# Five changes of instruction order in the two-layer hybrid encoder: merge copies and weights, last convolution, gate functions, retention's rotations, Hyena's turn

## The chip, the core and the metric

The kernel runs on one core of one Trainium2 chip. Time is device microseconds (us) of that core, as the median of repeated executions of the compiled program. One execution was recorded by the hardware profiler, and its rows are what "the trace" means below. The engines are TensorE (PE in the rows; PEld is its weight load), VectorE (DVE), ScalarE (ACT), GpSimd (POOL) and SyncE (SP, which issues most DMAs). Each engine works through its own queue in order; between engines there are semaphores.

## The reference

The reference is a trunk of two layers over an input of 512 positions by 1024 channels, all in float32.

- Layer 0: RMSNorm, one input projection, then two mixers side by side. Mixer A is a bidirectional gated DeltaNet (4 heads of 128, short convolution over three positions on q, k and v, then per chunk and direction a unit lower triangular system is solved and a state is carried from chunk to chunk). Its gates are `beta = sigmoid(b)` and `g = -exp(a_log) * softplus(a + dt_bias)`. Mixer B is a mixture of three dilated windows with rotary embedding (8 heads of 64). Both outputs go through one output projection and are added to x.
- Layer 1: RMSNorm, one input projection, then mixer C, bidirectional retention with rotary embedding (4 heads), and mixer D, Hyena: a short convolution, products, and a long convolution by Fourier transforms with filters made by a small network. Output projection, residual.
- After each layer's mixers comes RMSNorm and a feed-forward block of width 2816: gate and up projections, a convolution of three positions on the gate, `silu(gate) * up`, and a projection back. A last RMSNorm ends it.

```python
m = a + jnp.eye(C)                       # DeltaNet, per chunk: unit lower triangular
sol = lax.linalg.triangular_solve(m, rhs, left_side=True, lower=True, unit_diagonal=True)
qkv = jax.nn.silu(dwconv(proj[..., : 3 * W], conv_w))
g = -jnp.exp(a_log) * jax.nn.softplus(a + dt_bias)
x = x + conv_ffn(rmsnorm(x, norm_ffn[layer]), ...)
```

## The kernel before, in words

Dense products keep float32 accuracy by splitting each operand into a high and a low part in a matmul-friendly float32 format: `whi`/`wlo` for weights, `hh`/`hl` for activations. `mm3` (lines 263 to 267) issues three matmuls per product: high-high, high-low, low-high. A weight arrives by a 512 KB DMA on SyncE into `raw` (three buffers), ScalarE makes the high part (line 253, or line 250 where a scale is applied, as in the mixer's output projection), VectorE the low part (line 254 or 251). `fetch` does this for one weight; `get(ahead)` fetches until `ahead` weights are ready, and hands out one. There are four buffers each for high and low parts.

The text of the program does not fix the order on an engine. A planner takes every instruction with its dependencies, estimates durations, and gives each engine its queue: among the instructions that it thinks ready, the one traced first. So an instruction written later can float ahead into a gap that the planner sees, and an estimate that is off shows as a wait on the chip. Two things hold the planner: `manual_schedule`, used for the start alone, and `issue_after(ins)`, which queues what a block traces on the engine of `ins` behind `ins` on that engine; it orders the queue and waits for nothing else, and leaves the other engines' instructions free.

PSUM has two groups of four banks: `acc` for projections and outputs, `wk` for small work. A projection can start only when the reader of an older tile in its bank is done.

In order of the program, the stages that the change touches:

- **Dilated stage** (`dilated`, from line 505). Sixteen units of score, softmax, transposition (line 537, copied out at line 539 by ScalarE and VectorE in turn) and product with v (line 548). `DPROJ` says behind which unit the later q and k projections are issued, and, in its last two entries, behind which step of the loop the next piece of the generator `gates` is traced: steps 10 and 15 of 0 to 18.
- **Gates** (`gates`, from line 604). A generator in pieces: a projection of 32 columns; then four transpositions and a chain of small functions on 128 x 32 values, exponentials and logarithms on ScalarE (lines 631, 634, 639, 640, 642), the rest on VectorE; then cumulative sums by small matmuls (lines 659, 660), their exponential (line 662) and copies. The third piece is traced behind the first projection of the DeltaNet stage, since each `tile` there calls `next(gates)` (line 733).
- **DeltaNet preparation** (`delta_prep`, from line 707). Twelve projections of q, k and v columns, each with a convolution (`conv3`: ScalarE takes the middle tap at line 363, VectorE the outer taps at lines 366 and 367), Silu (lines 737 and 756), and a transposition a projection later (line 715). Then the Z projection (`proj_tok`, named `pt` in rows), in the same four `acc` banks.
- **Diagonal blocks** (`deltanet`, lines 814 to 865). The 32 x 32 diagonal blocks of the triangular systems are collected in `Bt`, transposed to `L` (line 851, VectorE), inverted by sixty dependent VectorE instructions (lines 858 and 859), and transposed back into `Y1` and `Y2` (lines 864 and 865; `vs` is the memory of `Y2`). Beside this TensorE works on the Z projection and on five units of the dilated mixer's output projection (`fill`, rows named `oacc` with `yh` and `yl`, twelve matmuls each).
- **Merge** (lines 886 to 933). Blocks of 32 are merged to 64 and then to 128: a first product (`m32`, line 890, row name `m`), its sums copied by both engines (line 892), the inverted diagonal blocks copied into `P` (line 895, eight copies, VectorE and ScalarE by direction), one filler unit, a second product (`m32b`, line 900), its sums copied (line 902); then transpositions (`vp`, lines 912 and 913) and the same for 64 (`m64`, lines 921 and 923, and `m64b`, lines 930 and 932), with another filler unit. The scan over chunks follows, with the last unit.
- **Retention** (`retention`, from line 1028). Four projections of q and k; `rope_in` copies each out of PSUM (line 458, ScalarE) and swaps halves by four DMAs on SyncE; `rope_out` multiplies and adds (lines 467 to 469, GpSimd and VectorE) and writes high and low parts (lines 474 and 475). `rot(i)` is the i-th `rope_out`. The projection of v (`pt`) follows in the same four banks.
- **Hyena** (`hyena`, from line 1212). Twelve projections (`hap`) with convolutions; u, made of the two first of each three, is transposed (`turn`, line 1240) during the third, ahead of the K step `HT`.
- **Feed-forward** (`ffn`, from line 408): 22 columns in each layer, with two projections (`gup`) each, and the projection back (`oacc`).

Of the kernel before, what the change touches and what calls it, by code (L numbers as in the profile page):

```python
# [10 lines left out]
AF = mybir.ActivationFunctionType  # L11
ALU = mybir.AluOpType
# [3 lines left out]
S = 512  # L16
# [47 lines left out]
def bc(ap, shape):  # L64
    return ap.to_broadcast(shape)


class Norm:


    out = None
# [91 lines left out]
class K:  # L163
# [194 lines left out]
    def conv3(self, out, ps, w, o, b=None):  # L358

        nc = self.nc  # L360
        w0, w1, w2 = [w[:, k:k + 1] for k in o]
        if b is None:
            nc.scalar.activation(out, ps, AF.Copy, scale=w1)
        else:
            nc.scalar.activation(out, ps, AF.Identity, scale=w1, bias=b)
        nc.vector.scalar_tensor_tensor(out[:, 1:], ps[:, :S - 1], w0, out[:, 1:], op0=ALU.mult, op1=ALU.add)
        nc.vector.scalar_tensor_tensor(out[:, :S - 1], ps[:, 1:], w2, out[:, :S - 1], op0=ALU.mult, op1=ALU.add)  # L367

    def rows_t(self, pool, srcs, nm):

# [231 lines left out]
    def gates(self, dp, n):  # L602
# [27 lines left out]
        V.tensor_scalar(e, gt[:, :, 0:8], -1.0, 80.0, op0=ALU.mult, op1=ALU.min)  # L630
        nc.scalar.activation(e, e, AF.Exp)
        V.tensor_scalar(e, e, 1.0, None, op0=ALU.add)
        nl = T("gnl")
        nc.scalar.activation(nl, e, AF.Ln)
        V.reciprocal(beta, e)
        V.tensor_tensor(y, gt[:, :, 8:16], bc(row[:, 0:1, :], [128, 4, 8]), op=ALU.add)
        V.tensor_scalar(u, y, -1.0, None, op0=ALU.mult)
        V.tensor_tensor(u, u, y, op=ALU.min)
        nc.scalar.activation(e, u, AF.Exp)
        nc.scalar.activation(row[:, 1, :], row[:, 1, :], AF.Exp)  # L640
        V.tensor_scalar(u, e, 1.0, None, op0=ALU.add)
        nc.scalar.activation(g, u, AF.Ln)
        V.tensor_scalar(u, u, -1.0, None, op0=ALU.add)
        V.tensor_scalar(g2, u, 0.0, None, op0=ALU.is_equal)
        V.tensor_tensor(u, u, g2, op=ALU.add)
# [5 lines left out]
        V.tensor_scalar(y, y, 0.0, None, op0=ALU.max)  # L651
        V.tensor_tensor(g, g, y, op=ALU.add)
        V.scalar_tensor_tensor(g, g, -1.0, bc(row[:, 1:2, :], [128, 4, 8]), op0=ALU.mult, op1=ALU.mult)
        yield
        gp = self.wk((128, 128), "gp")
        for d in range(2):
# [47 lines left out]
    def delta_prep(self, dp, n, gates, K_, Q_, V_, Z_):  # L704

        nc, I = self.nc, self.I
        V = nc.vector
        cw = self.rows_t(dp, [I["dn_conv_w"][0].rearrange("k (f p) -> (k f) p", p=128)], "dncw")
        pend = []

        def turn():
            sl, which, h = pend.pop(0)
            tp = self.wk((128, 4, 128), "tp")
            for cc in range(4):
                nc.tensor.transpose(tp[:, cc, :], sl[:, cc * 128:(cc + 1) * 128], self.ident)
            if which == 2:
                nc.scalar.copy(V_[:, :, h, :], tp)
                return
            ss = self.sm.tile([128, 4], F32, tag="dss", name="dss", bufs=2)
            jk = self.sm.tile([128, 4, 128], F32, tag="jk", name="sq", bufs=1)  # L720
            nc.scalar.activation(jk, tp, AF.Square)
            V.tensor_reduce(ss, jk, axis=AX.X, op=ALU.add)
            r = self.sm.tile([128, 4, 1], F32, tag="dr", name="dr", bufs=2)
            self.rstd(ss, 1.0, 1e-6, r[:, :, 0])
            if which == 0:
                nc.gpsimd.tensor_scalar(r, r, 128 ** -0.5, None, op0=ALU.mult)
            V.tensor_tensor((Q_, K_)[which][:, :, h, :], tp, bc(r, [128, 4, 128]), op=ALU.mult)

        def tile(which, h):
            f = which * 4 + h  # L730
            ap = self.acc(nm="ap")
            self.last_ap = self.proj_t(self.get(), n, ap).ins
            next(gates, None)
            c = self.vscr.pop(0) if which == 2 else self.s2("c")
            self.conv3(c, ap, cw, (f, 12 + f, 24 + f))
            if which < 2 or h == 0:
                nc.scalar.activation(c, c, AF.Silu)
            pend.append((c, which, h))

        for i, (which, h) in enumerate([(w_, h_) for w_ in (1, 0) for h_ in range(4)]):  # L740
            tile(which, h)
            if i:
                turn()
            if i > 5:
                yield
        tile(2, 0)
        turn()
        yield
        turn()
        tile(2, 1)  # L750
        yield
        tile(2, 2)
        yield
        tile(2, 3)
        for c, _, _ in pend:
            nc.scalar.activation(c, c, AF.Silu)
        turn()
        turn()
        yield
        turn()  # L760
        yield
        self.proj_tok(n, lambda t, a: nc.scalar.activation(Z_[:, t, :], a, AF.Silu))
        yield

    def deltanet(self, n, gates, yb, nxt):
        nc, I = self.nc, self.I
        V = nc.vector
        with ExitStack() as ctx:
# [79 lines left out]

            X = self.xp.tile([128, 32, 32], F32, tag="xn", name="L")
            Xf = X.rearrange("p a b -> p (a b)")  # L850
            V.transpose(Xf, Bt.rearrange("p m s -> p s m"))
            tm = dp.tile([128, 256], F32, name="tm")
            for _ in prep:
                pass
# [11 lines left out]
            self.x = self.new_x()  # L866
            for t in range(NT):
                self.load_x(t)
            wb = [self.get() for _ in range(4)]
            units = [(t, half) for half in range(2) for t in range(NT)]  # L870

            def fill(n):
# [15 lines left out]
            for m in range(16):  # L888
                for (d, s, o), p in zip(pairs, ps):
                    nc.tensor.matmul(p[blk(o), m, :], P[d][blk(s), m, blk(o)], Yv[d][blk(s), :, 16 * d + m], start=True, stop=True, tile_position=(32 * s, 32 * o))  # L890
            for i, ((d, s, o), p) in enumerate(zip(pairs, ps)):
                (V.tensor_copy if i % 2 else nc.scalar.copy)(T32[blk(o)], p[blk(o)])
            for q in range(4):
                for d in range(2):
                    (V.tensor_copy, nc.scalar.copy)[d](P[d][blk(q), :, blk(q)], Yu[d][blk(q), :, 16 * d:16 * d + 16].rearrange("p a m -> p m a"))
            fill(FILLS[1])
            ps = [self.wk((128, 16, 32), "m32b") for _ in pairs]
            for m in range(16):
                for (d, s, o), p in zip(pairs, ps):
                    nc.tensor.matmul(p[blk(s), m, :], T32[blk(o), m, :], Yu[d][blk(o), :, 16 * d + m], start=True, stop=True, tile_position=(32 * o, 32 * s))  # L900
            for i, ((d, s, o), p) in enumerate(zip(pairs, ps)):
                (V.tensor_copy if i % 2 else nc.scalar.copy)(P[d][blk(s), :, blk(o)], p[blk(s)])
            fill(FILLS[2])

            half = lambda b: slice(64 * b, 64 * b + 64)
# [122 lines left out]
    def retention(self, n, order):  # L1028
        nc, I = self.nc, self.I
        V = nc.vector  # L1030
        with ExitStack() as ctx:
# [8 lines left out]
            def rot(i):  # L1040
                which, s = i // 2, i % 2
                qk[which, s] = self.rope_out(rp, rope, *rin[i][:2], which == 0, f"r{which}{s}", 1)

            for i in range(4):
                if i == 3:
                    self.proj_t(self.get(), n, ps[3])
                rin.append(self.rope_in(rp, ps[i], 1.0 if i // 2 else 0.125, self.rope_room() if i % 2 else None))
                if i < 2:
                    rot(i)
            with self.tc.issue_after(rin[3][2].ins):  # L1050
                rot(2)
                rot(3)
            v = rp.tile([128, NT, 512], F32, name="rv")
            Z = rp.tile([128, NT, 512], F32, name="rz")
            self.proj_tok(n, lambda t, a: nc.scalar.copy(v[:, t, :], a))
# [274 lines left out]

WB = 4
TPD = lambda k: k.acc
DPROJ = (0, 2, 5, 8, 10, 15)
DAT = (1, 2)
FILLS = (5, 1, 0, 1, 0, 0, 0, 0, 1)
VT = (0, 1)
# [1 line left out]
G4 = 10  # L1338
FILLC = 1
IA = 3  # L1340
HT = 6
HSKIP = (1, 3)


# [56 lines left out]
```

## Time and profile before

| | |
|---|---|
| median of 3 runs | 1330.83 us (1330.3 to 1331.14) |
| the profiled execution | 1330.02 us |
| its span, first to last instruction | 1328.2 us |
| VectorE, ScalarE, GpSimd busy | 750.6, 531.6, 147.4 us |
| mean granted TensorE clock | 0.996 |
| DMA | 123.61 MB, mean 93 GB/s |

A row of a timeline gives the start, the duration, the engine, the line of the kernel, the operation, what it writes and reads, and the shape; in square brackets the idle time of the engine before it, and what ended that. A row of a group gives a count, the busy time, the mean duration in ns, and the idle time before. A row of waits gives who waited for whom, the total in us, the number of times and the longest. A row of a stretch (A:B) gives the length and the busy time of each engine, then the granted TensorE clock as a share, the DMA share and GB/s. Matmuls overlap: one of 512 columns lasts 0.39 us in the rows, and the next starts 0.23 us after it. The name behind an arrow is the releaser that came last by the profile, and can be wrong where that engine had long been done.

### The profile page before, as it was taken

To read this page: it belongs to the slowest core of one execution; us is meant where nothing else is said; L and a number is where in the kernel's file an instruction comes from. 1 tells how busy PE (TensorE), PEld (TensorE's weight loads), DVE (VectorE), ACT (ScalarE), POOL (GpSimd) and SP (SyncE) were. 2 spreads that over 40 slices of the span, in tenths; PEclk is the share of its full clock that TensorE was granted. 3 is DMA by queue.
4 is the path that set the end of the run, shared out by engine and by line. 5 is a ranking of instruction groups with operands and counts; after the bars stand their busy time and mean duration, and the time that the engine had idled before them with its cause. 6 is when DMAs were issued, how large, how long until landed. Compare 5 with 4: busy or idle time off the path is not lost.

```text
span 1328.2 us, 17628 instructions
## 1 busy us (share of the span) xinstructions
PE 1304.8 (98%) x6977; PEld 1093.2 (82%) x6977; DVE 750.6 (57%) x1085; ACT 531.6 (40%) x840; POOL 147.4 (11%) x176
## 2 busy tenths in 40 slices
PE   7999999999999999999999999999999999999997
PEld 6877788878988888888889787888898888888886
DVE  6777559957754433444436837869754442244432
ACT  4566648344433331233326424442443331133332
POOL 3354120003000000000001200124100000000002
PEclk9999999989999999999999999999999999999999
DMA  7531113411333333333323513330243333333321
GB/s 219 129 94 36 51 32 96 143 49 60 93 113 96 95 95 95 96 95 97 98 91 101 162 48 92 102 94 18 67 140 95 95 95 96 87 117 98 95 79 64
DMA packets 161025, 123.61 MB, mean 93 GB/s; under 512 B 6985, under 2 KB 134477, under 8 KB 160944
## 3 DMA queue, kind: packets, MB, share of 16 engines
q1 hardware_dynamic: 160798, 122.43, 31.2%
q8 instruction: 55, 0.90, 0.3%
q14 instruction: 26, 0.21, 0.1%
q10 hardware_dynamic: 146, 0.07, 0.0%
HBM read 117.23 MB, written 2.10 MB: 90 GB/s over the span
## 4 chain that ended last, share of the span: by engine, by line
PE 84%; DVE 7%; ACT 4%; issue 2%; DMA 1%; POOL 1%; SPq 0%; POOLq 0%; ACTq 0%; DVEq 0%
PE gup L266 11%; PE gup L265 11%; PE gup L267 11%; PE oacc L265 7%; PE oacc L267 7%; PE oacc L266 7%; PE hap L267 2%; PE pt L265 2%; PE hap L265 2%; PE hap L266 2%; PE pt L267 2%; PE pt L266 2%; PE ap L267 1%; PE ap L265 1%; PE ap L266 1%
## 5 line engine op out<-in xcount | busy, mean ns | idle before, releaser
L254 DVE TENSOR_TENSOR wlo<-raw,whi 128x1024 fp32r<-128x1024 f32 x191 | 236.0, 1237 | 304.1 <-ACT whi L253 299.3
L253 ACT CAST whi<-raw 128x1024 fp32r<-128x1024 f32 (+1 forms) x197 | 206.7, 1050 | 427.6 <-PE gup L266 186.8
L265 PE MATMUL gup<-hh,whi 128*128 128x512 f32 x656 | 255.2, 389 | 0.0
L266 PE MATMUL gup<-hl,whi 128*128 128x512 f32 x656 | 255.2, 389 | 0.0
L267 PE MATMUL gup<-hh,wlo 128*128 128x512 f32 x656 | 255.2, 389 | 0.0
L267 PEld LDWEIGHTS gup<-hh,wlo 128*128 128x128 f32 x656 | 123.1, 188 | 25.6
L265 PEld LDWEIGHTS gup<-hh,whi 128*128 128x128 f32 x656 | 123.2, 188 | 25.6
L266 PEld LDWEIGHTS gup<-hl,whi 128*128 128x128 f32 x656 | 123.2, 188 | 25.4
L265 PE MATMUL oacc<-whi,ghi 128*128 128x512 f32 x352 | 137.1, 389 | 0.0
L267 PE MATMUL oacc<-whi,glo 128*128 128x512 f32 x352 | 137.0, 389 | 0.0
L266 PE MATMUL oacc<-wlo,ghi 128*128 128x512 f32 x352 | 136.9, 389 | 0.0
L267 PEld LDWEIGHTS oacc<-whi,glo 128*128 128x128 f32 x352 | 66.1, 188 | 13.7
L265 PEld LDWEIGHTS oacc<-whi,ghi 128*128 128x128 f32 x352 | 66.1, 188 | 13.7
L266 PEld LDWEIGHTS oacc<-wlo,ghi 128*128 128x128 f32 x352 | 66.1, 188 | 13.6
L430 DVE TENSOR_TENSOR sl<-gup,sl 128x512 f32<-128x512 f32 x42 | 29.0, 692 | 81.8 <-PE gup L267 81.8
L315 DVE TENSOR_TENSOR x<-oacc,x 128x512 f32<-128x512 f32 x64 | 43.4, 685 | 49.3 <-PE oacc L267 49.2
L429 ACT ACTIVATE sl<-c 128x512 f32<-128x512 f32 x44 | 27.8, 632 | 89.2 <-DVE c L367 89.2
L265 PE MATMUL first<-hh,whi 128*128 128x256 f32 x192 | 54.9, 288 | 0.0
L266 PE MATMUL first<-hl,whi 128*128 128x256 f32 x192 | 54.5, 284 | 0.2 <-DVE hl L226 0.2
L267 PE MATMUL first<-hh,wlo 128*128 128x256 f32 x192 | 54.3, 283 | 0.0
L265 PE MATMUL pt<-whi,hh 128*128 128x512 f32 x128 | 50.2, 392 | 2.6 <-ACT room L458 1.7
L104 POOL TENSOR_SCALAR ss<-ss 128x1 f32<-128x1 f32 x16 | 5.0, 312 | 429.3 <-ACT jk L102 429.3
(422 smaller groups left out, 2346.4 us busy)
## 6 DMA issues: line engine op xcount, KB each, us to landing
raw<-in_ffn_w_in_dram SPq DMA_DIRECT2D x88, 512.0 KB, 3.8
raw<-in_ffn_w_out_dram SPq DMA_DIRECT2D x44, 512.0 KB, 3.9
raw<-in_ab_w_in_dram SPq DMA_DIRECT2D x28, 512.0 KB, 3.9
raw<-in_cd_w_in_dram SPq DMA_DIRECT2D x24, 512.0 KB, 4.3
x<-in_x_dram SPq DMA_DIRECT2D x16, 256.0 KB, 5.0
raw<-in_ab_w_out_dram SPq DMA_DIRECT2D x8, 512.0 KB, 3.8
raw<-in_cd_w_out_dram SPq DMA_DIRECT2D x8, 512.0 KB, 3.8
rs<-rt SPq DMA_DIRECT2D x32, 64.0 KB, 2.0
```

Of the source, the lines that this page charges most:

```text
L104: nc.gpsimd.tensor_scalar(ss[:, 1:2], ss[:, 0:1], s, EPS, op0=ALU.add, op1=ALU.add)
L253: self.nc.scalar.copy(hi, raw)
L254: (self.nc.gpsimd if self.pool_lo else self.nc.vector).tensor_tensor(lo, raw, hi, op=ALU.subtract)
L265: mm(out, a[0], b[0], start=start, stop=False)
L266: mm(out, a[0], b[1], start=False, stop=False)
L267: return mm(out, a[1], b[0], start=False, stop=stop)
L315: self.nc.vector.tensor_add(xs, acc, xs)
L429: nc.scalar.activation(sl, c, AF.Silu)
L430: nc.vector.tensor_mul(sl, up, sl)
```

## The change

No arithmetic changes. It has these parts:

1. Gates: the logarithm of `e` works on a copy (VectorE) and stands behind the other functions; `DPROJ` ends in 18 instead of 15, so that the second piece is traced behind the whole dilated stage; one more `yield` lets the third piece follow the second projection of the DeltaNet stage instead of the first.
2. Last convolution: the transposition to `L` is queued behind the last instruction of the last convolution, on VectorE.
3. Merge: the diagonal copies are queued behind the copies of the first sums on both engines, and VectorE takes six of the eight; the fourth `get` for the filler units asks for one weight ahead instead of two, and two `fetch` calls, queued behind the copies of the second sums, take its place and that of the next.
4. Retention: ScalarE's part of `rot(1)` is queued behind the copy of the fourth projection, as that of `rot(2)` and `rot(3)` was.
5. Hyena: `HT` is 7 instead of 6.

```diff
-        nc.vector.scalar_tensor_tensor(out[:, :S - 1], ps[:, 1:], w2, out[:, :S - 1], op0=ALU.mult, op1=ALU.add)
+        return nc.vector.scalar_tensor_tensor(out[:, :S - 1], ps[:, 1:], w2, out[:, :S - 1], op0=ALU.mult, op1=ALU.add)
...
-        nl = T("gnl")
-        nc.scalar.activation(nl, e, AF.Ln)
         V.reciprocal(beta, e)
...
+        nl = T("gnl")
+        V.tensor_copy(nl, e)
         nc.scalar.activation(e, u, AF.Exp)
         nc.scalar.activation(row[:, 1, :], row[:, 1, :], AF.Exp)
         V.tensor_scalar(u, e, 1.0, None, op0=ALU.add)
         nc.scalar.activation(g, u, AF.Ln)
+        nc.scalar.activation(nl, nl, AF.Ln)
...
+        yield
         yield
         gp = self.wk((128, 128), "gp")
...
-            self.conv3(c, ap, cw, (f, 12 + f, 24 + f))
+            self.last_conv = self.conv3(c, ap, cw, (f, 12 + f, 24 + f)).ins
...
-            V.transpose(Xf, Bt.rearrange("p m s -> p s m"))
+            with self.tc.issue_after(self.last_conv):
+                V.transpose(Xf, Bt.rearrange("p m s -> p s m"))
...
-            wb = [self.get() for _ in range(4)]
+            wb = [self.get(1 + (i < 3)) for i in range(4)]
...
-            for i, ((d, s, o), p) in enumerate(zip(pairs, ps)):
-                (V.tensor_copy if i % 2 else nc.scalar.copy)(T32[blk(o)], p[blk(o)])
-            for q in range(4):
-                for d in range(2):
-                    (V.tensor_copy, nc.scalar.copy)[d](P[d][blk(q), :, blk(q)], Yu[d][blk(q), :, 16 * d:16 * d + 16].rearrange("p a m -> p m a"))
+            out = [(V.tensor_copy if i % 2 else nc.scalar.copy)(T32[blk(o)], p[blk(o)]).ins
+                   for i, ((d, s, o), p) in enumerate(zip(pairs, ps))]
+            with self.tc.issue_after(out[2]), self.tc.issue_after(out[3]):
+                for q in range(4):
+                    for d in range(2):
+                        (nc.scalar.copy if d and q % 2 else V.tensor_copy)(P[d][blk(q), :, blk(q)], Yu[d][blk(q), :, 16 * d:16 * d + 16].rearrange("p a m -> p m a"))
...
-            for i, ((d, s, o), p) in enumerate(zip(pairs, ps)):
-                (V.tensor_copy if i % 2 else nc.scalar.copy)(P[d][blk(s), :, blk(o)], p[blk(s)])
+            out = [(V.tensor_copy if i % 2 else nc.scalar.copy)(P[d][blk(s), :, blk(o)], p[blk(s)]).ins
+                   for i, ((d, s, o), p) in enumerate(zip(pairs, ps))]
+            with self.tc.issue_after(out[2]), self.tc.issue_after(out[3]):
+                for _ in range(2):
+                    self.fetch()
...
-                if i < 2:
+                if i == 0:
+                    rot(0)
+            with self.tc.issue_after(rin[3][2].ins):
+                for i in range(1, 4):
                     rot(i)
-            with self.tc.issue_after(rin[3][2].ins):
-                rot(2)
-                rot(3)
...
-DPROJ = (0, 2, 5, 8, 10, 15)
+DPROJ = (0, 2, 5, 8, 10, 18)
...
-HT = 6
+HT = 7
```

## The prediction

> **What bounds the kernel.** I read the page first, its span, busy times and costliest groups.
>
> ```profile
> span 1328.2 us, 17628 instructions
> PE 1304.8 (98%) x6977; PEld 1093.2 (82%) x6977; DVE 750.6 (57%) x1085; ACT 531.6 (40%) x840; POOL 147.4 (11%) x176
> L254 DVE TENSOR_TENSOR wlo<-raw,whi 128x1024 fp32r<-128x1024 f32 x191 | 236.0, 1237 | 304.1 <-ACT whi L253 299.3
> L265 PE MATMUL gup<-hh,whi 128*128 128x512 f32 x656 | 255.2, 389 | 0.0
> ```
>
> TensorE has work in 98% of the span. The change removes no matmul, so all it can win is TensorE's waiting, some 23 us, and whatever TensorE does more slowly around a wait. So the next view is that of waits, for TensorE, matmuls first and then weight loads:
>
> ```profile
> PE m32b L900 <- DVE s L892: 1.9, 2, 1.4
> PE pt L265 <- ACT room L458: 1.7, 1, 1.7
> PE m32b L900 <- ACT s L892: 1.2, 1, 1.2
> PE pt L265 <- DVE scr L367: 0.9, 1, 0.9
> PE op L548 <- ACT pT L539: 0.9, 1, 0.9
> PE tp L1240 <- ACT hsh L225: 0.6, 1, 0.6
> ```
> ```profile
> PEld m L890 <- DVE vs L865: 0.4, 1, 0.4
> ```
>
> Six rows, five places, 7.2 us: merge sums, retention's fourth projection, the last convolution, the gates' functions, the hyena turn. Each edit points at one of them. The seventh row matters as much: when the merge starts, TensorE is already waiting for VectorE's transposed inverse, so time won shortly ahead of it may be handed back there.
>
> The sum is made against the profiled execution, 1330.02 us (span 1328.2 and 1.8 around it). That is 0.8 below the median of the three runs, 1330.83, so the total is carried over with 0.8 added.
>
> **Gates.** ScalarE at the end of the dilated stage (start, duration):
>
> ```profile
> 134.39 1.28 ACT L634 ACT_TABLE_LOAD   x1
> 135.68 0.23 ACT L634 ACTIVATE gnl<-ge 128x32 f32<-128x32 f32 x1
> 135.93 1.28 ACT L639 ACT_TABLE_LOAD   x1
> 137.36 0.57 ACT L539 COPY pT<-tp 128x512 f32<-128x512 f32 x1
> ```
>
> The last probabilities' copy (L539) stands behind two table loads and three small functions, and the last product waits 0.9. DPROJ's 18 puts the second piece of the gates behind all of the stage, and the copy of e with a late Ln makes Exp, Exp, Exp, Ln, Ln of what was Exp, Ln, Exp, Exp, Ln: two of 1.28 us loads fewer. The copy then finds ScalarE free: -0.9. The added tensor_copy is one of VectorE's small ones, hidden beside the projections. The piece's four transposes merely move behind the products. Its two loads of eight values on SyncE move with it; at worst they lengthen a chain that now has a whole projection (24 matmuls of 0.23, 5.5) to spare. Who is late next? The extra yield moves the cumulative sums and their Exp from behind the first projection to behind the second, and with them a pair of table switches:
>
> ```profile
> 150.33 0.63 ACT L737 ACTIVATE scr<-scr 128x512 f32<-128x512 f32 x1
> ```
> ```profile
> 152.79 0.60 PE L715 MATMUL tp<-ident,scr 128*128 128x128 f32 x4
> ```
>
> Today Silu ends at 150.96 and its reader starts at 152.79: 1.8 to spare. One projection later a Square of 0.6 comes in between; 1.2 remains, so I take nothing. Bounds: -0.9, and +0.5 if the turn gives back 1.4 (below).
>
> **Last convolution.** VectorE, at the start and at the end of its elimination chain; then TensorE:
>
> ```profile
> 228.91 2.06 DVE L851 STREAM_TRANSPOSE L<-Bt 128x1024 f32<-128x1024 f32 x1
> 262.43 1.21 DVE L865 STREAM_TRANSPOSE vs<-L 128x1024 f32<-128x1024 f32 x1
> ```
> ```profile
> 263.97 0.23 PE L890 MATMUL m<-Y,P 32*32 32x32 f32 x2
> ```
>
> The transposition of 2.06 was queued ahead of the convolution's second half, which holds a PSUM buffer that the Z projection wants. Swapped, the buffer is free some 2 us earlier and TensorE's 0.9 goes. But VectorE does the same two instructions in the same time, so its sixty-step elimination starts and ends as before; vs is ready at 263.64 and m starts at 263.97. TensorE arrives 0.9 earlier and waits 0.9 longer. I take 0; ends 0 and -0.9 (if a filler unit of the output projection is pulled ahead of m).
>
> **Merge.** The largest term. First the stretches 270 to 275 and 275 to 280 with the granted clock (third column from the right), then groups of VectorE, TensorE and ScalarE from the start of m to the end of m64b, 263.9 to 286:
>
> ```profile
> 270.00:275.00 5.00, 2.96 (x129) 2.61 (x130) 3.59 (x5) 1.14 (x3) 0.24 (x1) 0.72 0.44 135
> 275.00:280.00 5.00, 4.83 (x38) 2.90 (x37) 1.88 (x5) 1.86 (x6) 0.80 (x1) 0.60 0.27 105
> ```
> ```profile
> L315 DVE TENSOR_TENSOR x<-oacc,x 128x512 f32<-128x512 f32 x5 | 3.4, 683 | 1.0 <-PE oacc L267 0.9
> L251 DVE SCALAR_TENSOR_TENSOR wlo<-raw,dnw,whi 128x1024 fp32r<-128x1024 f32 x2 | 2.6, 1278 | 0.7 <-ACT whi L250 0.7
> L895 DVE COPY P<-vs 32x512 f32<-32x512 f32 x4 | 2.4, 602 | 0.0
> L913 DVE COPY s<-vp 64x256 f32<-64x256 f32 x4 | 1.5, 417 | 3.1 <-PE vp L912 3.1
> L892 DVE COPY s<-m 32x512 f32<-32x512 f32 x2 | 1.4, 693 | 0.1
> L902 DVE COPY P<-m32b 32x512 f32<-32x512 f32 x2 | 1.4, 692 | 1.3 <-PE m32b L900 1.3
> ```
> ```profile
> L895 ACT COPY P<-Y 32x512 f32<-32x512 f32 x3 | 3.4, 1128 | 0.0
> ```
> ```profile
> 271.12 1.42 DVE L892 COPY s<-m 32x512 f32<-32x512 f32 x2
> ```
> ```profile
> 274.52 0.80 PE L265 MATMUL oacc<-whi,yh 128*128 128x512 f32 x1
> 280.07 2.36 PE L921 MATMUL m<-s,P 64*64 64x64 f32 x64
> 282.36 0.50 PE L265 MATMUL oacc<-whi,yh 128*128 128x512 f32 x1
> 283.95 2.08 PE L930 MATMUL m64b<-P,s 64*64 64x64 f32 x64
> ```
>
> m is done at about 265.9, but its sums are copied by VectorE only at 271.12, behind four diagonal copies, two weights' low halves (L251) and x additions. TensorE stands idle 3.1 us, and behind that the granted clock falls to 0.72 and 0.60: a filler's matmul takes 0.80, where those of gup take 0.39.
>
> Afterwards the sums go first, while the filler unit of twelve matmuls runs, so m32b has no wait and there is no reason for the lower clock. What bounds then? Of the eight diagonal copies VectorE gets six (was four), since ScalarE needs 1.13 for one. Its queue from the end of m to what the first half of m64 reads: sums 2 x 0.69, diagonals 6 x 0.60, one addition 0.68, L902 2 x 0.69, the two weights 2 x 1.28, now directly ahead of L913, and two L913 at 0.42: 10.5. With 0.3 of hand-overs m64 starts at 265.9 + 10.8 = 276.7, not 280.07: -3.4. The six filler matmuls between m64 and m64b (282.36 to 283.95, 1.6) are by then spent, in time that TensorE has to spare; I keep 0.4 for the wait that they covered: -1.2. Together -4.6. ScalarE's two diagonals and two weights are shorter than this. Bounds: -2.0, if the weights and diagonals hold L913 up for another 2.6 (two more weights' worth); -6.5, if neither the wait (3.1) nor the low clock (5 x 0.28 and 5 x 0.40, so 3.4) leaves anything.
>
> The weights prepared here are wanted only by the mixer's output projection past 316, so lateness costs nothing; SyncE's raw loads behind them move some 5 us, with FFN weights due far later.
>
> **Retention.** ScalarE, and TensorE's row behind it:
>
> ```profile
> 735.48 1.26 ACT L474 CAST r<-rt 64x512 fp32r<-64x512 f32 x2 [2.49 <-DVE rt L469]
> 738.90 1.26 ACT L474 CAST r<-room 64x512 fp32r<-64x512 f32 x2 [1.08 <-DVE room L469]
> 740.18 0.60 ACT L458 ACTIVATE room<-rqk 128x512 f32<-128x512 f32 x1
> ```
> ```profile
> 740.83 0.50 PE L265 MATMUL pt<-whi,hh 128*128 128x512 f32 x1 [1.68 <-ACT room L458]
> ```
>
> L458 frees the PSUM buffer. It stands behind rotation 1's casts, which wait for VectorE. With those queued behind it, it has only rotation 0's casts ahead, to 736.7, and ends at 737.3; TensorE wants it at 740.83 - 1.68 = 739.1, and even a weight's cast of about a microsecond in between would not make it late: -1.7. The four DMAs on SyncE that follow L458 go 2 to 5 us earlier. Rotation 1's cast becomes late by one instruction of 0.6; heads 2 and 3 read it twenty microseconds on. Bounds -1.7, and -1.0 if VectorE's or ScalarE's order leaves 0.7.
>
> **Hyena turn.** VectorE, then TensorE:
>
> ```profile
> 884.88 0.68 DVE L1254 TENSOR_TENSOR u<-vx 128x512 f32<-128x512 f32 x1
> ```
> ```profile
> 885.70 0.52 PE L1240 MATMUL tp<-ident,u 128*128 128x128 f32 x3 [0.64 <-ACT hsh L225]
> ```
>
> The page names hsh, but u ends at 885.56, just ahead of tp: VectorE is what it waits for. HT 7 puts three more matmuls (3 x 0.23) ahead: -0.6. Bounds -0.6, and 0 if u is pushed back as far as tp.
>
> **Sum.** 0.9 + 0 + 4.6 + 1.7 + 0.6 = 7.8. 1330.02 - 7.8 = 1322.2; with 0.8, 1323.0.
>
> **Rivals.** *VectorE eats the merge.* Only 2.0 there: the wait moves from m32b to vp and m64. For: the queue above makes VectorE the bound already, and two of its copies more in ahead would do it. Against: over the same stretch, to 280.07, VectorE took 14.2, with 3.1 of idling at L913 that the new order fills. Gain 5.2, 1325.6.
> *Fillers cover all.* The filler is pulled ahead of m, so the convolution's 0.9 stays won and TensorE bounds the merge: 0.9 + 0.9 + 6.5 + 1.7 + 0.6 = 10.6, 1320.2. Against: VectorE's 10.5 queue doesn't shrink when TensorE is early.
> *Table switches reach the second projection.* If ScalarE needed two more 1.28 between Exp and Silu, 2.6 against 1.2 to spare, the turn waits 1.4: 1324.4. Against it: in the rows each function starts 1.29 after its load starts. [...]
> *Orders elsewhere shift.* The planner builds each engine's queue from estimated times, so five edits can move others; a new wait of over 5 cancels the gain: about 1330. For: rows such as L851's place show it estimates wrongly by a microsecond. Against: the stages between have no wait now.
> *Slower: FFN columns.* A moved weight preparation (1.24) lands ahead of a column's additions and recurs in 44 columns. It decides from 0.18 a column (7.8 in all); at 0.25 it is 11, so 1334. Against: gup's 656 matmuls have 0.0 idle before them, and VectorE is idle 304 us at L254 alone.
> *Not done as said* would be an order already in force; the trace shows each of the five orders otherwise, so none.
>
> **Numbers.** Forecast 0.50, VectorE 0.20, fillers 0.12, switches 0.05, orders elsewhere 0.08, FFN 0.05. The likeliest gives 1323.0, by itself 1321 to 1325. The range takes in the first four: below, the fillers' 10.6 and 0.1 for each of the five restarts (0.50 for 0.39 in retention's row), 11.1, 1319.7; above, the VectorE case with retention and the turn at their small ends (0.9 + 2.0 + 1.0 = 3.9, 1326.9). About 0.2% (2.7 us) is what a measurement can tell: faster 0.87, same 0.08, slower 0.05.
>
> **What would show it.** Right: no L458, L367 or L539 row among TensorE's waits; L892 directly behind m on both engines; clock 1.00 through the merge; m still waiting on L865, now by 0.9 longer; m64 some 3.4 earlier relative to m. Wrong: L913 standing behind L251 for over 3 us, a wait at gp or at the second turn, idle before gup, or a halved clock again.

## The result, and the profile after

The changed kernel takes 1322.37 us (median of 6 runs, 1322.2 to 1322.88), the kernel before 1330.99 beside it (6 runs, 1330.3 to 1332.83): a ratio of 0.9933, 95% interval 0.992 to 0.9946. The profiled execution took 1322.2 us, 7.8 less than that of before. The granted clock differs between executions, and the time with it: 32 further executions of the kernel before took 1328.5 to 1328.8 us at 0.998, 1329.0 to 1330.8 at 0.996 or 0.997, and 1332.0 to 1332.9 at 0.993 or 0.994, while all six of the changed kernel had 0.998 or 0.999.

Line numbers behind the gates' functions are 2 to 7 higher from here on: m is L893, the sums' copies L894, the diagonal copies L899, m32b L904, vp L919, m64 L928, m64b L937; the edits of an experiment shift them by a few more.

From the page of the changed kernel, its span and busy times (the work is what it was):

```profile
span 1320.1 us, 17630 instructions
PE 1302.8 (99%) x6977; PEld 1092.6 (83%) x6977; DVE 751.6 (57%) x1088; ACT 527.1 (40%) x837; POOL 146.4 (11%) x176
```

Rows of TensorE's waits in the changed kernel (us in total, times, longest). Of the five places that the prediction went for, three are gone from the view, and the two others have shrunk: the merge's wait has moved on to vp, at 0.2, and the Hyena turn (L1247) has 0.2 left. m now waits visibly for vs:

```profile
PE tp L537 <- ACT pT L539: 0.8, 1, 0.8
PE vnp L973 <- DVE s L959: 0.6, 1, 0.6
PE m L893 <- DVE vs L868: 0.4, 1, 0.4
PE vp L919 <- DVE P L905: 0.2, 1, 0.2
PE tp L1247 <- ACT hsh L225: 0.2, 1, 0.2
```

(The wait at L537 is not the one of the gates: it ends at 83.4 us, in the first part of the dilated stage, and was 0.8 before the change too.) The stretches that answer to those shown of before, with the granted clock third from the right:

```profile
265.00:270.00 5.00, 5.00 (x142) 3.98 (x140) 4.85 (x9) 3.43 (x5) 0.41 (x1) 1.00 0.02 3
270.00:275.00 5.00, 4.80 (x44) 2.90 (x42) 4.40 (x6) 4.01 (x7) 0.63 (x1) 1.00 0.35 109
275.00:280.00 5.00, 5.00 (x123) 4.68 (x124) 3.70 (x8) 1.72 (x3) 0.41 (x1) 1.00 0.73 209
```

The clock is whole throughout, and TensorE is busy for 14.8 of these 15 us. Rows of VectorE through the merge, in order of time (diagonal copies and additions to x between them are left out):

```profile
261.14 1.20 DVE L868 STREAM_TRANSPOSE vs<-L 128x1024 f32<-128x1024 f32 x1
264.46 1.42 DVE L894 COPY s<-m 32x512 f32<-32x512 f32 x2 [0.35 <-PE m L893]
270.20 1.42 DVE L905 COPY P<-m32b 32x512 f32<-32x512 f32 x2
272.12 0.42 DVE L920 COPY s<-vp 64x256 f32<-64x256 f32 x1 [0.50 <-PE vp L919]
272.57 2.48 DVE L251 SCALAR_TENSOR_TENSOR wlo<-raw,dnw,whi 128x1024 fp32r<-128x1024 f32 x2
275.08 1.08 DVE L920 COPY s<-vp 64x256 f32<-64x256 f32 x3
```

The sums are copied at 264.46, directly behind m, where they came at 271.12 before. But the two weights (L251) stand between the first copy of vp and the other three. What that does shows on TensorE, where m64 runs in two pieces:

```profile
274.89 1.14 PE L928 MATMUL m<-s,P 64*64 64x64 f32 x16
276.40 2.07 PE L928 MATMUL m<-s,P 64*64 64x64 f32 x48
278.31 2.08 PE L937 MATMUL m64b<-P,s 64*64 64x64 f32 x64
```

Where the time came from is read by setting the starts of the same instructions on TensorE beside each other; where the difference grows, time was won. The two traces start their first projection at 15.51 and 15.59, so 0.08 is put to the gates' row. (Differences are taken before rounding.)

| TensorE's instruction | before | after | difference | won since the row above |
|---|---|---|---|---|
| first projection behind the dilated stage | 139.42 | 138.02 | -1.39 | 1.47 (gates) |
| last of the Z projection | 250.05 | 247.88 | -2.18 | 0.79 (convolution) |
| first filler matmul behind m | 265.90 | 264.40 | -1.50 | -0.68 (given back at m) |
| start of m64 | 280.07 | 274.89 | -5.18 | 3.68 (merge) |
| start of m64b | 283.95 | 278.31 | -5.64 | 0.46 (merge) |
| first product of retention | 761.85 | 754.19 | -7.66 | 1.99 (retention; 0.03 on the way) |
| end of the Hyena projections | 887.09 | 879.02 | -8.07 | 0.41 (HT) |

### The profile page after: what moved, and what is told of

It reads as the page before. It is cut to its first block, busy times and chain, and to the rows that moved or that the text cites. A ratio compares the mean times of both kernels' runs of the same rounds, so it can differ in the third digit from the quotient of the medians.

```text
span 1320.1 us, 17630 instructions
## 1 busy us (share of the span) xinstructions
PE 1302.8 (99%) x6977; PEld 1092.6 (83%) x6977; DVE 751.6 (57%) x1088; ACT 527.1 (40%) x837; POOL 146.4 (11%) x176
## 4 chain that ended last, share of the span: by engine, by line
PE 87%; DVE 6%; ACT 2%; DMA 1%; issue 1%; SPq 1%; POOL 1%; POOLq 0%; ACTq 0%; DVEq 0%
PE gup L266 11%; PE gup L267 11%; PE gup L265 11%; PE oacc L266 7%; PE oacc L267 7%; PE oacc L265 7%; PE pt L267 2%; PE pt L265 2%; PE pt L266 2%; PE first L266 2%; PE first L267 2%; PE first L265 1%; PE ap L266 1%; PE ap L265 1%; PE ap L267 1%; PE hap L265 1%
```

## Experiments

Every kernel below is the changed one with the edit that its diff shows. Times are medians of 5 runs (10 for e2). The interval of a ratio is some 1.7 us to either side, so differences of half a microsecond between these kernels are read from the traces, and the times only say whether they fit. Where two traces are set on each other, the start of the first projection (15.59 in the changed kernel) is taken out. In e2 and e7 that isn't all: there 0.6 and 0.3 us more are lost before anything that the edits touch (in e7 the first projection behind the dilated stage starts at 138.39, 0.37 later than in the changed kernel, of which 0.10 is there at the start); why isn't shown.

**e2, all of the merge undone.**

```diff
-            wb = [self.get(1 + (i < 3)) for i in range(4)]
+            wb = [self.get() for _ in range(4)]
...
-            with self.tc.issue_after(out[2]), self.tc.issue_after(out[3]):
...
-                        (nc.scalar.copy if d and q % 2 else V.tensor_copy)(P[d][blk(q), ...
+                        (V.tensor_copy, nc.scalar.copy)[d](P[d][blk(q), ...
...
-                for _ in range(2):
-                    self.fetch()
```

> Undone: all edits of the merge (sums copied in program order with the diagonal blocks, four of these on each engine, weights fetched ahead of the merge as before). Theory (the merge is worth what TensorE's milestones shifted by between the start of m and the end of m64b, 4.1): 1326.5, within 0.4, with m32b waiting about 3 again and the granted clock below 1 in the stretch behind it. Rival (part of that shift is the convolution's 0.9, which could only be used because the merge became shorter): +5.0, 1327.4.

Measured: 1326.46, ratio to before 0.9974 (0.9964 to 0.9983), so 4.1 above the changed kernel. In the trace m64b comes 4.66 later (282.97 for 278.31), of which 0.3 is there already at the filler unit behind m. The waits at m32b are back, and the low clock with them:

```profile
PE m32b L903 <- DVE s L895: 1.9, 2, 1.5
PE m32b L903 <- ACT s L895: 1.4, 1, 1.4
```
```profile
270.00:275.00 5.00, 3.69 (x129) 2.83 (x129) 3.55 (x6) 1.15 (x2) 1.04 (x1) 0.62 0.45 134
```

The merge is half of the whole gain, and its gain is its own: the time is the theory's 1326.5 and not the rival's 1327.4, so the convolution's share isn't in it. Its edits are two, the place of the weights and the place of the diagonal copies; e3 and e4 keep one each.

**e3, only the copies' order** (weights fetched ahead of the merge again: `wb` as in e2, the two `fetch` gone).

> Only half of the merge's edits: the sums stay ahead of the diagonal blocks (and six of these on VectorE), but the two weights are fetched ahead of the merge as before, so both low halves (2 x 1.24) stand ahead of the sums on VectorE. Theory (the filler unit of 4.7 gives the queue slack, and either edit alone takes enough out of the way of the sums): sums copied by about 268.3, ahead of m32b's start at 269.2; vp starts some 2.4 later than in the changed kernel, but its copies no longer stand behind the weights, so m64 ends at about the same time: 1322.4, within 0.6. Rival (the two edits add up, about half of 4.1 each): 1324.4.

Measured: 1326.31, 0.9967 (0.9955 to 0.998): by the median nothing is left of the merge's gain, and both expectations fall. But the profiled execution is the quickest of the five, 1324.86 at a clock of 0.998 (the others took 1325.18, at 0.998, and 1326.31 to 1326.92, at 0.996 or 0.997), so its trace covers 2.7 (1324.86 beside the changed kernel's 1322.2) of the 3.9 that lie between the medians; the rest goes with a lower clock that no trace of this kernel shows. VectorE of this kernel:

```profile
262.64 1.27 DVE L251 SCALAR_TENSOR_TENSOR wlo<-raw,dnw,whi 128x1024 fp32r<-128x1024 f32 x1
264.42 1.29 DVE L251 SCALAR_TENSOR_TENSOR wlo<-raw,dnw,whi 128x1024 fp32r<-128x1024 f32 x1
266.34 1.42 DVE L894 COPY s<-m 32x512 f32<-32x512 f32 x2
272.90 1.42 DVE L905 COPY P<-m32b 32x512 f32<-32x512 f32 x2
```

The sums are there at 267.8 (266.34 + 1.42), by the theory's 268.3, and m32b waits 0.4 for them, where the theory had no wait. But everything behind is 2.7 later (L905 at 272.90 for 270.20), and vp waits for it:

```profile
274.37 0.67 PE L916 MATMUL vp<-ident,P 64*64 64x64 f32 x16 [2.46 <-DVE P L905]
275.96 3.89 PE L925 MATMUL m<-s,P 64*64 64x64 f32 x64
```

Then came what the theory had left out. It expected that the copies of vp, with no weights between them, would make up for the 2.4. They came in time, but m64 took 3.89 where it takes 2.36 at the whole clock (its row in e11, below): three stretches, one during it and a short one on either side, show the clock at 1.00, 0.50 and 1.00 again.

```profile
275.80:276.10 0.30, 0.30 (x6) 0.21 (x5) 0.30 (x2) 0.30 (x1) 0.00 (x0) 1.00 0.00 0
276.20:279.50 3.30, 3.30 (x62) 3.30 (x61) 0.97 (x2) 0.58 (x1) 0.00 (x0) 0.50 0.00 0
279.70:280.00 0.30, 0.30 (x4) 0.23 (x3) 0.11 (x1) 0.20 (x1) 0.00 (x0) 1.00 0.00 0
```

So 2.7 of late copies became a wait of 2.46, and behind the wait came a clock that cost 1.5 more; part of both is covered by filler matmuls, and m64b starts 3.1 later than in the changed kernel.

**e4, only the weights' place** (diagonal copies as in e2, in program order, four on each engine).

> The other half: the two weights stay behind the sums of m32b, but the diagonal blocks are copied in program order again, four on each engine, ahead of the sums of m. Theory (the filler unit covers them): on VectorE the sums end at about 267.9, on ScalarE, behind four copies of 1.13, at about 266.9, both ahead of m32b's start at 269.2; so 1322.4, within 0.5, no wait at m32b. Rival (the copies ahead of the sums are what held m32b up, as the change's own words have it): about +2, 1324.4, with m32b waiting on the sums.

Measured: 1322.73, 0.9942 (0.993 to 0.9955): nearly all of the gain is there. ScalarE, then VectorE, of this kernel (its trace lies 0.86 later from the first projection on):

```profile
261.99 4.44 ACT L898 COPY P<-Y 32x512 f32<-32x512 f32 x4 [11.39 <-DVE Y L867]
266.45 1.18 ACT L895 COPY s<-m 32x512 f32<-32x512 f32 x2
```
```profile
267.40 1.42 DVE L895 COPY s<-m 32x512 f32<-32x512 f32 x2
```

The sums stand behind the diagonal copies on both engines, and are done at 267.6 and 268.8 all the same, when TensorE comes out of the filler unit at 268.1. m32b waits 0.44, where the theory had no wait, and m64b is 0.4 later than in the changed kernel (1.23 less the 0.86). So of the merge's two edits the weights' place brings some 4 by itself, and the copies' order 0.4 on top of it. Without the weights' place the order brings nothing by the medians (1326.31 for 1326.46), and 1.8 between the two profiled executions, 0.5 of which lies ahead of m; whether the rest is the copies or the clock isn't shown, since e2's trace has 6.8 us at half clock and e3's 3.4.

**e10, e2 with TensorE kept busy.** Diff against e2:

```diff
             fill(FILLS[1])
+            p = self.acc(nm="warm")
+            for _ in range(24):
+                nc.tensor.transpose(p[:, :128], self.ident, self.ident)
```

> The kernel with all the merge's edits undone (1326.5 in its own run), plus 24 transpositions of the identity that nobody reads, between the filler unit and m32b: some 3 us of TensorE work in the time in which it waits for the sums. Work is added, nothing moved. Theory (the loss in the merge is the wait for the copies; the halved clock behind it is hidden by VectorE's queue but for some 0.5): the granted clock stays at 1.00 and the time falls by 0.3 to 0.7, to 1325.8 to 1326.2. Rival (the lower clock is itself a large part of the loss, up to the 3.4 of the prediction's bound): 1323 to 1325.

Measured: 1324.98, 0.9955 (0.9942 to 0.9967), a span of 1324.1 beside e2's 1324.8. TensorE, and then the stretches:

```profile
267.23 2.78 PE L902 MATMUL warm<-ident 128*128 128x128 f32 x24
270.58 0.22 PE L906 MATMUL m32b<-vs,s 32*32 32x32 f32 x1 [0.36 <-DVE s L895]
271.30 0.22 PE L906 MATMUL m32b<-Y,s 32*32 32x32 f32 x1 [0.44 <-DVE s L895]
```
```profile
273.00:273.30 0.30, 0.30 (x17) 0.21 (x7) 0.04 (x1) 0.08 (x1) 0.00 (x0) 1.00 0.16 44
273.40:276.70 3.30, 3.30 (x10) 1.76 (x9) 1.25 (x2) 1.34 (x3) 1.04 (x1) 0.50 0.45 161
276.80:277.10 0.30, 0.30 (x11) 0.28 (x11) 0.00 (x0) 0.00 (x0) 0.00 (x0) 1.00 0.03 14
```

The waits at m32b shrink to 0.8, since work that is of no use to anybody stands in their place, and the halved clock to one stretch of 3.4 (e2's stretches read 0.50 from 271.30 to 277.90, and 1.00 up to 271.10 and from 278.10 on). Neither expectation holds wholly: the clock of the theory did not stay at 1.00, and the median gained 1.5, just inside the rival's 1323 to 1325. The profiled execution, the longest of its five, gained 0.8, of which only 0.36 lies between the filler unit behind m and m64b (17.92 for e2's 18.28). Two of the five were granted 0.999, as most of the changed kernel's, and took 1324.98 and 1325.3: 1.2 to 1.5 less than e2's median and 2.6 to 2.9 more than the changed kernel's. So the larger part of the merge's 4.1 is the queue of copies (with the added work in it), and the lower clock is some 1.2 to 1.5 of it. That is an estimate, since no trace of those two executions was kept.

**e11, the weights later still.**

The two `fetch` move from behind the copies of m32b to behind the second pair of copies of m64b, `out` being these:

```diff
-            with self.tc.issue_after(out[2]), self.tc.issue_after(out[3]):
-                for _ in range(2):
-                    self.fetch()
...
+            with self.tc.issue_after(out[0]), self.tc.issue_after(out[1]):
+                for _ in range(2):
+                    self.fetch()
```

> The two weights are fetched behind the copies of m64b instead of behind those of m32b; all else as changed. Their low halves (2.5 on VectorE) then no longer stand between the copies of vp, so m64 runs in one piece. Theory (TensorE has filler work in that time and is busy for 4.8 of the 5 us there, so little is left to win): 1322.0 to 1322.4, m64b 0.2 to 0.5 earlier. Rival (VectorE still holds up the merge, the prediction's 1.2 between m64 and m64b of which 0.5 came): -0.7 or more, 1321.6, m64b 0.7 earlier or more. Rival on the other side (the weights now stand ahead of the copies of sp, in the scan): +0.5 to +2.

Measured: 1322.58, 0.9936 (0.9924 to 0.9948), the same as the changed kernel. The trace shows that both rivals came true at once, with opposite signs:

```profile
273.19 2.36 PE L925 MATMUL m<-s,P 64*64 64x64 f32 x64
277.06 2.08 PE L934 MATMUL m64b<-P,s 64*64 64x64 f32 x64
282.58 2.02 PE L983 MATMUL sp<-s,s 128*128 128x128 f32 x16 [1.45 <-ACT s L975]
```
```profile
279.78 2.19 ACT L250 ACTIVATE whi<-raw,dnw 128x1024 fp32r<-128x1024 f32 x2
281.88 1.05 ACT L975 COPY s<-vnp 128x512 f32<-128x512 f32 x2
```

m64 runs in one piece and starts 1.70 earlier, m64b 1.25 (277.06 for 278.31): the two weights did hold the merge up. This move takes their 2.2 on ScalarE (L250) out of the way of the copies of vp along with the 2.5 on VectorE (L251), so it doesn't tell the two engines apart. Then the weights' high halves (L250) stand ahead of the copies of vnp on ScalarE, and the scan waits 1.45 for them; at the scan's end the kernel is 0.34 behind. The wait is moved, not removed.

**e5, e6, e7: the gates' three edits.** e5 undoes the place (DPROJ 15, one `yield`), e6 the order of the functions, e7 takes out the extra `yield` alone. The edits of e5 and of e6:

```diff
-DPROJ = (0, 2, 5, 8, 10, 18)
+DPROJ = (0, 2, 5, 8, 10, 15)
...
-        yield
```
```diff
+        nl = T("gnl")
+        nc.scalar.activation(nl, e, AF.Ln)
         V.reciprocal(beta, e)
...
-        nl = T("gnl")
-        V.tensor_copy(nl, e)
...
-        nc.scalar.activation(nl, nl, AF.Ln)
```

> Of the gates' edits only the order of the functions stays (Exp, Exp, Exp, Ln, Ln); the piece goes back to its old place in the dilated stage (DPROJ 15) and the extra step between it and the sums is gone. Theory (the place is what frees the last probabilities' copy): one table load of 1.28 and two functions still stand ahead of that copy on ScalarE, which starts by some 137.1 instead of 137.4 before the change, so 0.6 to 0.9 of the wait stays; +0.7 to +1.2, 1323.1 to 1323.6. Rival (the two table loads fewer are what counts): +0.2 at most, 1322.6.

> The other half: the piece stays behind the dilated stage (DPROJ 18, extra step), but the functions run as before, Exp, Ln, Exp, Exp, Ln, with two table loads of 1.28 more in the piece. Theory: the gates' chain ends 2.6 later, at about 147.1, and its reader gp comes at 149.6, so nothing waits: 1322.4, within 0.3. Rival (table switches reach the second projection: the turn or gp waits): +0.5 to +1.4, with a wait at gp or at the turn's tp.

> Only the extra step is taken out: the gates' cumulative sums gp stand one projection earlier on TensorE, at about 143.3, all else as changed. Theory (the gates' chain, now behind the dilated stage, ends at 144.5 on VectorE, so gp comes too early for it): TensorE waits about 1.2 at gp; +1.2, 1323.6. Rival (the step only moved work that nobody waits for): 0, 1322.4.

Measured: e5 1322.87 (0.9937, 0.9924 to 0.9951), e6 1322.23 (0.9933, 0.992 to 0.9945), e7 1322.72 (0.9937, 0.9924 to 0.9949). One row of TensorE's waits for each, of e5, e6 and e7:

```profile
PE op L548 <- ACT pT L539: 0.7, 1, 0.7
```
```profile
PE tp L716 <- ACT scr L738: 0.2, 1, 0.2
```
```profile
PE gp L660 <- DVE gg L654: 0.3, 1, 0.3
```

In e5 the wait for the last probabilities' copy is back at 0.7 of its 0.9, and the projections start 0.9 later (0.81 plus the 0.07 by which this trace is early), as the theory had it; the time lies between theory and rival. In e6 they start where the changed kernel's do. So the place alone frees the copy. The order alone, with two table loads of 1.28 fewer (three in the gates' functions before, L634, L639 and L642; one in the changed kernel, L643), wins 0.6 of the 1.47 that both won together, of which only 0.2 is waiting; with the place changed it adds nothing there. In e6 the second turn, which has 1.5 to spare in the changed kernel (Silu ends at 149.47, the turn starts at 150.96), waits 0.2, and the projections end 0.45 later (0.39 and 0.05): the rival of the table switches is real, but small. In e7 gp waits 0.3, not the 1.2 that the theory forecast, because the first projection ends at 144.1, its transpositions (rowp) included, and not at 143.3, and the planner put one more matmul and a transposition ahead of gp, which starts at 144.97; the projections end 0.7 later (0.77, less 0.10), of which 0.3 is the difference at the start and 0.4 lies behind gp.

**e1, the convolution undone** (the `issue_after(self.last_conv)` line).

> Undone: the convolution's second half no longer goes ahead of the block transposition (the transposition is issued without waiting for it); all else as in the changed kernel. Theory (the 0.9 that TensorE no longer waits at the Z projection is handed back at m, where VectorE's transposed inverse vs is next late): 0.9 of waiting behind L367 comes back, the wait of m on vs shrinks from 0.4 to nearly nothing, and the end moves by 0 to +0.3: 1322.4 to 1322.7. Rival (the conversion of this wait is a gain of its own): +0.8, so 1323.2, with m's wait unchanged.

Measured: 1322.57, 0.9942 (0.9928 to 0.9955). The wait behind the convolution is back, in TensorE's waits, and m's is gone from them:

```profile
PE pt L265 <- DVE scr L367: 1.0, 1, 1.0
```

The Z projection ends 0.76 later than in the changed kernel (0.74 and 0.02), and at m32b only 0.09 of that is left. What is won there is handed back at m, as the theory has it.

**e8, retention undone** (`rot(1)` ahead of the fourth read again), **e9, HT back at 6.**

> Undone: retention's rotation 1 stands ahead of the fourth projection's read of its sums again. Theory (that read, L458, frees the PSUM buffer for the projections behind it, and is held up by the casts of rotation 1): the wait behind L458 of 1.7 returns, and with the weight load and restart around it TensorE's milestones shift by 2.0: 1324.4, within 0.3. Rival (the prediction's size, the wait alone): 1324.1; rival (other work fills the place): 1322.4.

> Undone: HT back at 6, so three matmuls fewer stand ahead of the hyena turn. Theory: the wait at that turn returns to 0.6 from 0.2, so +0.4 there, and at the end 1322.4 to 1322.8. Rival (the prediction's size): +0.6, 1323.0. Both are below what five rounds resolve in the time; the turn's wait in the trace decides.

Measured: e8 1323.89, 0.9948 (0.9935 to 0.996); e9 1322.51, 0.9935 (0.9922 to 0.9947). The wait of each in TensorE's view, e8 and then e9:

```profile
PE pt L265 <- ACT room L458: 1.7, 1, 1.7
```
```profile
PE tp L1247 <- ACT hsh L225: 0.6, 1, 0.6
```

In e8 the first product of retention comes 1.99 later (1.82, and the trace is 0.17 early by then). In e9 the turn's wait is 0.6 instead of 0.2, and the end of the Hyena projections moves by 0.37 from where they start: both traces as the theory had them. e8's time, 1.5 above the changed kernel's, falls 0.2 short of the theory's range; e9's can't tell.

**e12, four edits alone:** the weights' place, the gates' place with its step, retention, HT.

> Only four edits stay: the weights behind the sums of m32b, the gates' piece with its extra step behind the dilated stage, retention's rotation behind the fourth read, HT at 7. Undone together: the convolution ahead of the transposition, the sums ahead of the diagonal blocks with their 6 to 2 division, and the order of the gates' functions. Theory (each of these three brought 0.4 or less by itself): 1322.4 to 1323.1. Rival (they cover for each other, and without all of them the waits of before come back): 1324 or more.

Measured: 1323.13, 0.994 (0.9927 to 0.9954). Its waits show the three edits that are missing, each at its own place and none over 0.9:

```profile
PE pt L265 <- DVE scr L367: 0.9, 1, 0.9
PE m32b L901 <- DVE s L893: 0.4, 1, 0.4
PE tp L716 <- ACT scr L738: 0.2, 1, 0.2
```

TensorE ends 0.95 later than in the changed kernel; the sum of the three single ones (e1 0.34, e4 0.44, e6 0.29) is 1.07. They do not cover for each other: four edits bring 7.2 to 7.9 by the medians (1323.13 beside 1330.37 and 1330.99), and the other three the rest, which the medians alone can't resolve. No kernel among the twelve is measurably quicker than the changed one.

## Why the prediction was right

**What bounds, and the list of places:** right. Five places of waiting were named, and the time came from those five and the stretch of low clock; no other stage moved by more than 0.15.

**Gates, 0.9 forecast:** 1.47 came. The step was right and a term was missing: the product behind the wait also ran slowly. It took 1.43 before the change (the last sixteen matmuls) where its neighbours take 1.09; afterwards two such products run in one go. Before, and then after:

```profile
135.97 1.09 PE L548 MATMUL op<-pT,dv 128*64 128x128 f32 x16
137.98 1.43 PE L548 MATMUL op<-pT,dv 128*64 128x128 f32 x16 [0.91 <-ACT pT L539]
```
```profile
135.68 1.97 PE L548 MATMUL op<-pT,dv 128*64 128x128 f32 x32
138.02 0.48 PE L265 MATMUL ap<-hh,whi 128*128 128x512 f32 x1
```

Row by row: the last 32 matmuls went from 3.44 (135.97 to 139.41) to 1.97, so 1.47 was won: 0.91 of idle time, 0.34 of slow running, and 0.22 because one run of 32 takes less than two of 16 (1.97 for twice 1.09). The slow running isn't part of every wait, and its cause is not shown: in e5, behind 0.72 of waiting, the last sixteen take 1.09. The two table loads were put down as part of this gain; e6 shows that with the new place they belong elsewhere, to the second turn, for which the prediction took nothing because 1.2 remained. With the new order that is right; without it 0.2 of waiting comes in (e6), so the loads removed are what keeps the turn free.

**Last convolution, 0:** right, for the reason given (e1). TensorE reaches m 0.54 ahead of the end of vs, where it came 0.33 behind it, so 0.87 earlier against it; forecast was 0.9. One reading was off: that TensorE was already waiting for vs before the change. The row is one of a weight load, and its 0.4 was hidden: m started 0.32 behind the start of the last filler matmul (263.65 to 263.97), as m32b does in the changed kernel (267.03 to 267.35), where nothing waits.

**Merge, 4.6:** 4.14 came, by 3.68 at m64 (forecast 3.4) and 0.46 up to m64b (forecast 1.2). The second term was mis-sized: the six filler matmuls are spent ahead, as forecast, but m64 itself now stands in two pieces behind L251. The first term's size came out (from the start of the filler unit behind m, 264.40, to m64 it is 10.5; the prediction had 10.8 from the same point, 265.9), but its reason was half right. The prediction let the sums' place ahead of the diagonal blocks remove m32b's wait, with the weights as the queue's other part; e4 and e3 show that moving the weights is all but enough (m32b still waits 0.44), and that moving the sums alone leaves the medians where they were. With the weights ahead, VectorE's copies are late by 1.9 (the sums) to 2.7 (those of m32b) even so, and the wait only goes from m32b to vp. That the two weights set the start of m64 is borne out by e11 (1.70 earlier without them there); that it is VectorE's half of them, as the prediction has it, fits the second piece of m64, which starts 0.24 behind VectorE's last copy of vp (276.16), but isn't shown: the first piece stands behind vp and filler matmuls with no wait ahead of it.

**Retention, 1.7:** 1.99, again more than the idle time of 1.68. The rows count idle time from the end of the matmul ahead, but the next one normally starts 0.23 behind its start, and here it came 2.06 behind (738.77 to 740.83), and the one after 0.34 behind that. **Hyena turn, 0.6:** 0.41, since u is pushed back a little too: 0.18 of waiting stays.

**The sum:** 7.8 against 7.8 between the two profiled executions (8.1 between their spans). That is better than its terms, and so in part luck: gates and retention were 0.9 too low together, the merge and the turn 0.7 too high. The median came out 0.6 below the 1323.0 of the prediction, and the two medians lie 8.6 apart: the 0.8 that was carried over, as if both kernels' medians lay above their profiled executions alike, holds only for the kernel before, whose executions spread more.

**Rivals.** VectorE eating the merge is the nearest one in its mechanism (the weights hold up vp and m64, as e11 shows), but the new order is short enough that filler work hides it. The fillers did not move ahead of m, so the convolution's 0.9 did not stay. The table switches cost 0.2 at the turn in e6, not the 1.4 of the prediction. The FFN columns did not move: gup's first matmul and retention's come 5.67 earlier alike.

What stays open is the share of the halved clock in the merge. It is some 1.2 to 1.5 by e10, which also changes the waiting. The kernel before gives the same figure: those of its executions that were granted 0.998 took 1328.5 to 1328.8, 1.2 to 1.5 less than the profiled 1330.02 at 0.996. But where in them the clock was lower is not recorded, so both are estimates.

## What to carry to other kernels

When a copy is late because an engine's queue is full, look first for work in that queue that nobody needs soon (here two weights wanted 40 us later) and move that; the order among the copies that are needed mattered a tenth as much, and by the medians not at all without the first step. Before counting a wait as won, look at what the same engine waits for next, and at who stands behind the place to which work is moved: the convolution's 0.8 was handed back at m, and the weights moved once more (e11) won 1.25 and lost 1.6. A wait that is removed can be worth more than its idle time: here 1.47 for 0.91 and 1.99 for 1.68 where it went wholly and nothing was next late, but 0.79 for 0.91 at the convolution and 0.41 for 0.46 at the turn.

## What the hardware showed beside that

In four of the traces the clock was halved in the merge. Its length follows from the two stretches 270 to 275 and 275 to 280, as twice the 5 us times what they lack of 1.00: 6.8 us in the kernel before (0.72 and 0.60) and in e2 (0.62 and 0.70), 3.4 in e3 (1.00 and 0.66) and 3.4 to 3.5 in e10 (0.83 and 0.82, and the three stretches shown above). So two of the traces show about twice the length of the other two. How long TensorE had been idle does not tell the cases apart. In the 3.4 us just ahead of the drop, as long as the shorter of the two, TensorE was busy, by its rows, for 0.72 in the kernel before, 0.56 in e2, 1.55 in e3 and 2.60 in e10. In e11, in the 3.4 us up to the start of sp at 282.58, which hold its wait of 1.45, it was busy for 1.95, less than in e10, and the clock did not drop: the stretch 280 to 285 reads 1.00. What differs beside it is the kind of work: almost only transpositions (vp) in e3, almost only 32 x 32 matmuls (m32b) in e10, and 128 x 128 ones (vnp) in e11. What makes the clock drop isn't settled by these runs.
